# Conv gates moved to the end of each pass, parts split in place, and the last column block's weight quarters split once: a hybrid decoder step on one core

## The chip, the cores and the metric

The kernel runs on one core of a Trainium2 chip. The metric is the device time of one launch in microseconds, lower is better. TensorE (PE) does the matmuls, and its weight loads (PEld) overlap them; VectorE (DVE), ScalarE (ACT) and GpSimd (POOL) do the elementwise work; the transfers are issued on SyncE's queue (SP).

## What is computed

One layer of a decoder for 1024 prompt tokens and 64 sample tokens (8 sequences of 8), model width 2048. One input projection feeds three groups of heads; their results are joined and projected back:

```python
proj = jnp.einsum("bld,de->ble", x, w_in)
glu_a, glu_b, conv_gate, qkv, dn_gate, beta_in, decay_in, mem_q, mem_gate = jnp.split(proj, splits, axis=-1)
# conv group, 512 channels
hc, conv_state = causal_dwconv(glu_a * jax.nn.sigmoid(glu_b), conv_prev, conv_w)     # width 31
out_conv = jax.nn.silu(layer_norm(hc + conv_b, conv_ln_g, conv_ln_b)) * jax.nn.silu(conv_gate)
# delta-rule group, 8 heads of 128: short conv, gated delta rule, gated norm -> out_dn
# memory group, 4 heads of 128 over 256 memory tokens
p = jax.nn.softmax(jnp.einsum("blhd,bmhd->bhlm", mq, mem_k) * MEM_HEAD_DIM ** -0.5, axis=-1)
out_mem = jnp.einsum("blhm,bmhd->blhd", p, mem_v) * jax.nn.silu(mem_gate)
h = jnp.einsum("ble,ed->bld", jnp.concatenate([out_conv, out_dn, out_mem], axis=-1), w_out)
y = layer_norm(DEEPNORM_ALPHA * x + h, ln_g, ln_b)
```

The prompt's memory keys and values are themselves two projections (2048 to 512) of 256 memory tokens; the sample's come from a cache. The last conv rows, the delta states and the memory keys and values are outputs too.

## The kernel before, in words

Every large product is made of three matmuls on fp32r parts: a value is split into a rounded high part (an ACT copy) and the low rest (a DVE subtraction), and high x high, high x low and low x high are summed in PSUM. Weights come as raw tiles of 128 x 1024 (512 KB, a pool of 5, `rawp`), and `split_quarter` splits them in quarters of 128 x 512 into a ring of WB = 4 pairs (`wh`, `wl`); `ensure(n)` keeps n quarters split ahead of PE. The order of all loads is one list, `seq`, and a new load is issued when a raw tile is done.

**Passes.** The input projection runs twice over 52 columns of 128 outputs: pass 0 for 512 prompt tokens and the 64 samples (two banks of 288), pass 1 for the other 512 tokens. `ct_order` gives the order: 32 columns of the eight delta heads (k, q, v, gate each), 8 GLU columns (32 to 39), 4 conv gates (40 to 43), 4 memory queries (44 to 47), 4 memory gates (48 to 51). `gemm` emits a column; `finish` empties its PSUM banks behind the first matmul of the next and starts what hangs on it. Before column 44 of pass 0 `run_mem` projects the memory tokens: 192 matmuls on 32 quarters, and four more raw tiles that are split as well (`load_mem`). Pass 1 reads the keys and values back before its column 44 (`reload_mem`).

**Side work.** What follows the projection (delta chain, conv, attention) is a set of Python generators in `Side`. `tick`, called between groups of matmuls, takes them in turn and emits their next steps between PE's matmuls, if a planner's model of the engines' clocks (`Model`, `Proxy`) thinks that their inputs are there. `drain(cond)` ticks until a condition holds, without further matmuls of the column. All that is emitted is then fixed: each engine runs its instructions in this order. The conv (`gen_cgroup`) makes 31 tap instructions on DVE for each of four channel groups (with another 31 for the samples in pass 0), and holds back while the planned DVE clock is more than 1200 ns ahead of PE's. `gen_cln` then normalizes over the four groups' results `hc`, applies the gates `("g", j)`, and hands each to `put_mixed`. `gen_att` does a memory head: scores, softmax, product, for pass 0 also the samples against four cached key tiles (`kts`) and value tiles (`vts`); it multiplies by its gate and calls `put_mixed`.

**Buffers.** Most of these tiles share one pool of NW = 20 buffers (`W`, 128 x 576). Side work asks with `room(n)`, which as a rule leaves one free (KEEP); `finish` asks with `need()`, which drains side work until one is free, for each gate and query column. PSUM has four banks for columns (`m`) and four for side work (`s`).

**put_mixed** splits a finished result m of one of 16 groups into two new W tiles, high and low, and stores both to a DRAM tile `mixd[p][k]`, from where `load_mixed` brings them as stationary operands for the output.

**Output projection.** Two halves g (five tiles of tokens, the fifth the samples; then four), each in four column blocks cb of 512, 16 steps k each, three matmuls per tile and step (`out3`). `open_out`, at step 12 of the first block, drains all side work, frees the working pools and opens the output's (`Y`, among it 8 row buffers `y` of 128 x 2048). At a block's end `residual` adds alpha * x; `gen_ln` collects statistics, and after the fourth block normalizes in four pieces of 512 columns. After block 0 of the second half all side work is drained before the residuals. The last block of the second half is run in two phases: tiles 0 and 1 with all 16 steps, then tiles 2 and 3 with the same weights loaded and split again; of these the last HOLD = 10 steps are kept (six of them in `y` buffers, four in the ring), done for tile 2 first and then for tile 3. `finish_out` ends tiles 2 and 3 with DVE, ACT and POOL.

All engine calls are made in a helper, so nearly every row names line 88.

Of the kernel before, what the change touches and what calls it, by code (L numbers as in the profile page):

```python
# [16 lines left out]
P = 128  # L17
# [6 lines left out]
HOLD = 10  # L24
WB = 4
KEEP = 1
NSPLIT = 4 * 2 * 52 + 32 + 9 * KT
# [136 lines left out]
def hybrid_step(ctx, tc, I, O):  # L164
# [100 lines left out]
    for t in range(1, 52):  # L265
        if t == 44:
# [7 lines left out]
    seq += wo + wo + wo[24:]  # L274
# [46 lines left out]
    def split_quarter():  # L321
# [696 lines left out]
    convst = [dict(), dict()]  # L1018

    def gen_cgroup(p, j, a_sb, sg, psl):  # L1020
# [40 lines left out]
        for t in range(31):  # L1061
            while md.clk["DVE"] > md.clk["PE"] + 1200:
                yield "B"
# [349 lines left out]
    def run_mem(prev_fin):  # L1413
# [3 lines left out]
        bank = [(pss if i > 1 else psm).tile([P, 512], F32, tag="mmss"[i], name=nm("mm")) for i in range(4)]  # L1417
        for i in range(8):
# [18 lines left out]
            fr(2)  # L1437
        need(4)
# [53 lines left out]
    for t in range(1, 52):  # L1492
        if t == 44:
            run_mem(fin)
            fin = None
# [5 lines left out]
        fin = gemm(0, t, fin, refill_b if t == 51 else (lambda q: load_mem() if q == 2 else None) if t == 43 else None)  # L1501

    side.add(gen_gates(1, pb))
    for t in range(52):
        if t == 44:
# [59 lines left out]
    def gen_ln(rows, cb, st, y, bst, dst):  # L1565
# [6 lines left out]
        for cb in range(4):  # L1572
            cs = slice(512 * cb, 512 * cb + 512)
# [3 lines left out]
            yield  # L1577
            dve.tensor_tensor(out=yc, in0=yc, in1=gc, op=ALU.mult)
# [4 lines left out]
    def finish_out(ys, bst, xt, bank):  # L1583
        def chunk(i, cb):
            cs = slice(512 * cb, 512 * cb + 512)
            return ys[i][:, cs], Y["g"][:, cs], Y["b"][:, cs], O["y_p"][512 + i * P:512 + i * P + P, cs]

        def normalize(i, cbs):
            for cb in cbs:
                yc = chunk(i, cb)[0]  # L1590
                act.activation(out=yc, in_=yc, func=AF.Identity, scale=st[i][0], bias=st[i][1])

        def affine(i, cb, e0, e1):
            yc, gc, bb, dst = chunk(i, cb)
            e0.tensor_tensor(out=yc, in0=yc, in1=gc, op=ALU.mult)
            e1.tensor_tensor(out=yc, in0=yc, in1=bb, op=ALU.add)
            sp.dma_start(out=dst, in_=yc)

        def center(cb):
            yc, gc, bb, dst = chunk(3, cb)  # L1600
            dve.scalar_tensor_tensor(out=yc, in0=yc, scalar=st[3][2], in1=gc, op0=ALU.subtract, op1=ALU.mult)

        def rescale(cb):
            yc, gc, bb, dst = chunk(3, cb)
            dve.scalar_tensor_tensor(out=yc, in0=yc, scalar=st[3][0], in1=bb, op0=ALU.mult, op1=ALU.add)
            sp.dma_start(out=dst, in_=yc)

        st = {}
        for i in (2, 3):
            o, src = residual(P, 3, ys[i], bst[i], xt[i], bank[i])  # L1610
            dve.bn_stats(out=o, in_=src)
# [166 lines left out]
```

## Time and profile before

| what | value |
|---|---|
| runs | 2019.34, 2021.03, 4051.27 us; median 2021.03 |
| the profiled execution's own time | 2022.13 us |
| its span | 2020.4 us, 33329 instructions |
| PE busy | 1964.0 us (97%), 12172 matmuls |
| DVE, ACT, POOL busy | 1374.2 us (68%), 922.5 us (46%), 159.9 us (8%) |
| mean granted PE clock | 0.992 |
| moved by DMA | 257.35 MB, mean 127 GB/s |

How to read it: a row of the timeline gives start, length, engine, operation, output and inputs by tile names (buffer numbers left out), and in brackets how long the engine was idle before and what ended that. A row of busy times by stretch gives the stretch, its length, each engine's busy time with the number of its instructions in brackets, the granted PE clock (1.00 is full), the DMA engines' busy share and GB/s. A group row ends with busy time and mean ns, then the idle time before its members and what ended it. Tiles: `m` column banks, `mm` the memory block's, `om` the output's, `ps` side work's, `hc` the conv results.

### The profile page before, as it was taken

To read this page: it belongs to the slowest core of one execution; us is meant where nothing else is said; L and a number is where in the kernel's file an instruction comes from. 1 tells how busy PE (TensorE), PEld (TensorE's weight loads), DVE (VectorE), ACT (ScalarE), POOL (GpSimd) and SP (SyncE) were. 2 spreads that over 40 slices of the span, in tenths; PEclk is the share of its full clock that TensorE was granted. 3 is DMA by queue.
4 is the path that set the end of the run, shared out by engine and by line. 5 is a ranking of instruction groups with operands and counts; after the bars stand their busy time and mean duration, and the time that the engine had idled before them with its cause. 6 is when DMAs were issued, how large, how long until landed. Compare 5 with 4: busy or idle time off the path is not lost.

```text
span 2020.4 us, 33329 instructions
## 1 busy us (share of the span) xinstructions
PE 1964.0 (97%) x12172; PEld 1710.7 (85%) x12172; DVE 1374.2 (68%) x3423; ACT 922.5 (46%) x2279; POOL 159.9 (8%) x345
## 2 busy tenths in 40 slices
PE   8999999999999999899999999999999999999995
PEld 7999999999999979877888878888887788887784
DVE  6677767866878896455767777778995433338447
ACT  6555555555543244466545544553324522215124
POOL 6111101101101001000000000000101000000001
PEclk9999999999999999999999999999999999999998
DMA  6232333233323354374333333333332493376444
GB/s 209 85 110 74 100 110 110 73 102 110 102 95 101 99 183 131 110 231 150 120 97 99 100 99 106 110 100 95 101 115 77 139 375 103 102 245 206 140 132 150
DMA packets 114294, 257.35 MB, mean 127 GB/s; under 512 B 35281, under 2 KB 39633, under 8 KB 113873
## 3 DMA queue, kind: packets, MB, share of 16 engines
q1 hardware_dynamic: 114128, 255.22, 39.2%
q8 instruction: 96, 1.57, 0.3%
q14 instruction: 70, 0.57, 0.1%
HBM read 219.15 MB, written 36.01 MB: 126 GB/s over the span
## 4 chain that ended last, share of the span: by engine, by line
PE 44%; DVE 6%; issue 1%; ACT 1%; DMA 1%; SPq 0%; POOL 0%; DVEq 0%; ACTq 0%
PE m L88 22%; PE om L88 17%; PE ps L88 5%; DVE y L88 2%; DVE hc L88 1%; DVE wl L88 1%; DVE cv L88 1%; SPq L88 0%; DMA vts<-in_cv_dram 0%; ACT wh L88 0%; DMA ysc<-Y 0%; DVE held L88 0%; DMA mx<-mxl 0%; DMA out_y_p_dram<-y 0%; ACT gmh L88 0%
## 5 line engine op out<-in xcount | busy, mean ns | idle before, releaser
L88 PE MATMUL m<-x,wh 128*128 128x288 f32 (+1 forms) x4992 | 1228.1, 335 | 7.8 <-ACT wh L88 7.8
L88 PEld LDWEIGHTS m<-x,wh 128*128 128x128 f32 x4992 | 833.0, 189 | 84.2 <-issue 16.7
L88 PE MATMUL m<-x,wl 128*128 128x288 f32 (+1 forms) x2496 | 818.4, 328 | 1.7 <-DVE wl L88 1.7
L88 DVE TENSOR_TENSOR wl<-raw,wh 128x512 fp32r<-128x512 f32 x586 | 405.2, 698 | 294.5 <-ACT wh L88 285.6
L88 ACT CAST wh<-raw 128x512 fp32r<-128x512 f32 x586 | 357.3, 620 | 374.3 <-PE om L88 228.2
L88 PEld LDWEIGHTS m<-x,wl 128*128 128x128 f32 x2496 | 470.0, 188 | 37.4 <-DVE wl L88 2.9
L88 PE MATMUL om<-wh,x 128*128 128x512 f32 x1064 | 335.0, 391 | 0.0
L88 PEld LDWEIGHTS om<-wh,x 128*128 128x128 f32 x1064 | 200.7, 189 | 42.7 <-issue 1.0
L88 PE MATMUL om<-wl,x 128*128 128x512 f32 x564 | 220.8, 391 | 3.8 <-DVE wl L88 3.8
L88 DVE SCALAR_TENSOR_TENSOR hc<-u,cvc,hc 128x512 f32<-128x512 f32 x360 | 200.7, 595 | 2.4
L88 DVE TENSOR_TENSOR xt<-mb,X 128x8 f32<-128x8 f32 (+30 forms) x496 | 136.9, 276 | 10.5
L88 DVE SCALAR_TENSOR_TENSOR cv<-xr,qcw,cv 128x512 f32<-128x512 f32 (+1 forms) x216 | 128.9, 597 | 7.7
L88 PEld LDWEIGHTS om<-wl,x 128*128 128x128 f32 x564 | 106.5, 189 | 26.4 <-DVE wl L88 4.4
L88 ACT ACT_TABLE_LOAD x83 | 106.5, 1283 | 44.2 <-DVE smz L88 30.1
L88 DVE TENSOR_REDUCE X<-xt 128x4 f32<-128x8 f32 (+30 forms) x496 | 110.2, 222 | 10.6
L88 ACT ACTIVATE oi<-ps,GT 128x128 f32<-128x128 f32 x56 | 20.6, 368 | 210.1 <-DVE r L88 207.7
L88 ACT ACTIVATE jk<-ps 128x128 f32<-128x128 f32 x128 | 33.3, 275 | 51.8 <-PE ps L88 51.7
L88 ACT COPY xr<-m 128x288 f32<-128x288 f32 (+3 forms) x96 | 33.3, 396 | 20.5 <-PE m L88 20.0
L88 ACT ACTIVATE cv<-cv 128x512 f32<-128x512 f32 x48 | 30.3, 631 | 19.5 <-DVE cv L88 19.2
L88 PEld LDWEIGHTS ps<-S,cv 128*128 128x128 f32 x224 | 32.0, 190 | 4.7 <-DVE S L88 2.2
L88 PE MATMUL ps<-S,cv 128*128 128x128 f32 x224 | 34.4, 276 | 1.1 <-DVE S L88 1.1
L88 DVE SCALAR_TENSOR_TENSOR y<-xt,om 128x512 f32<-128x512 f32 (+1 forms) x36 | 24.2, 682 | 16.4 <-PE om L88 13.7
(318 smaller groups left out, 1817.4 us busy)
## 6 DMA issues: line engine op xcount, KB each, us to landing
raw<-in_wt_dram SPq DMA_DIRECT2D x208, 512.0 KB, 3.8
raw<-in_wo_dram SPq DMA_DIRECT2D x72, 512.0 KB, 3.9
x<-mx SPq DMA_DIRECT2D x16, 576.0 KB, 8.2
mb<-ysc SPq DMA_DIRECT2D x128, 64.0 KB, 2.2
mx<-mxh SPq DMA_DIRECT2D x32, 256.0 KB, 4.8
mx<-mxl SPq DMA_DIRECT2D x32, 256.0 KB, 4.9
xt<-in_xp_dram SPq DMA_DIRECT2D x32, 256.0 KB, 4.4
x<-mx SPq DMA_DIRECT2D x16, 512.0 KB, 3.6
```

The lines of the kernel that those rows point to most:

```text
L88: r = fn(**kw)
```

## The change

1. The order of columns: memory queries are now columns 40 to 43, memory gates 44 to 47, conv gates 48 to 51. The memory block, its loads, and the reload in pass 1 stand before column 40 instead of 44.
2. Within the memory block the conv taps are held back until the planned DVE clock is 500 ns behind PE's (`ahead`).
3. `put_mixed` writes the low part over m, and asks for one W buffer instead of two.
4. The last column block's weights are loaded and split once for both phases: its 16 quarters are kept, 8 in `y` buffers, 4 in the ring, 4 in raw tiles that no load needs any more. Tiles 0 and 1 take all 16 steps, then tile 2 all 16, then tile 3. That takes 8 loads of 512 KB and 16 quarters' splits out.
5. `gen_ln` normalizes in two pieces of 1024 columns, and holds back while the planned DVE clock is more than 1200 ns ahead.
6. The drain after block 0 of the second half ends with the first tile of the half before; a full drain stands after block 2. Tile 2 of the last block is ended as side work, and `finish_out` does tile 3 alone, on DVE and ACT, its last 512 columns in two halves.

```diff
-    order += [COL_CGATE + j for j in range(4)]
     order += [COL_MQ + j for j in range(4)]
     order += [COL_MGATE + j for j in range(4)]
+    order += [COL_CGATE + j for j in range(4)]
...
-        if t == 44:
+        if t == 40:
...
-    seq += wo + wo + wo[24:]
+    seq += wo + wo
...
-        j = nsplit[0] - 1 - (NSPLIT - (HOLD - WB))
-        if j < 0:
+        j = nsplit[0] - 1 - (NSPLIT - KT)
+        if j < 0 or 8 <= j < 12:
             hi, lo = (wp.tile([P, 512], F32R, tag=x, bufs=WB, name=nm(x)) for x in ("wh", "wl"))
-        else:
+        elif j < 8:
             if j % 2 == 0:
                 Y["held"] = Y["p"].tile([P, 2048], F32R, tag="y", bufs=8, name=nm("held"))
             hi, lo = (Y["held"][:, 1024 * (j % 2) + o:1024 * (j % 2) + o + 512] for o in (0, 512))
+        else:
+            assert nload[0] == len(seq)
+            t = rawp.tile([P, 1024], F32R, tag="raw", name=nm("held"))
+            hi, lo = t[:, 0:512], t[:, 512:1024]
...
-        yield from room(2)
-        parts = [W([P, NTOK[p]], F32R, name=n, held=True) for n in ("mxh", "mxl")]
-        act.copy(out=parts[0], in_=m)
-        dve.tensor_tensor(out=parts[1], in0=m, in1=parts[0].bitcast(F32), op=ALU.subtract)
-        fr()
-        yield tuple(parts)
+        yield from room(1)
+        hi = W([P, NTOK[p]], F32R, name="mxh", held=True)
+        act.copy(out=hi, in_=m)
+        parts = (hi, m.bitcast(F32R))
+        dve.tensor_tensor(out=parts[1], in0=m, in1=hi.bitcast(F32), op=ALU.subtract)
+        yield (hi, m)
...
+    ahead = [1200]
...
-            while md.clk["DVE"] > md.clk["PE"] + 1200:
+            while md.clk["DVE"] > md.clk["PE"] + ahead[0]:
                 yield "B"
...
+        ahead[0] = -500
         for i in range(8):
...
+        ahead[0] = 1200
         need(4)
...
-        for cb in range(4):
-            cs = slice(512 * cb, 512 * cb + 512)
+        for cb in range(2):
+            cs = slice(1024 * cb, 1024 * cb + 1024)
...
+            while md.clk["DVE"] > md.clk["PE"] + 1200:
+                yield "B"
...
+    def finish_out(y, bst, xt, bank):
+        o, src = residual(P, 3, y, bst, xt, bank)
+        dve.bn_stats(out=o, in_=src)
...
+        cols = [(0, 512), (512, 1024), (1024, 1536), (1536, 1792), (1792, 2048)]
...
+        center(cols[0])
+        dve.reciprocal(out=r, in_=r)
+        dve.scalar_tensor_tensor(out=nmr, in0=mean, scalar=-1.0, in1=r, op0=ALU.mult, op1=ALU.mult)
+        for c in cols[2:]:
+            yc = y[:, c[0]:c[1]]
+            act.activation(out=yc, in_=yc, func=AF.Identity, scale=r, bias=nmr)
+        for n, c in enumerate(cols):
+            yc, gc, bb = (t[:, c[0]:c[1]] for t in (y, Y["g"], Y["b"]))
+            if n < 2:
+                if n:
+                    center(c)
+                dve.scalar_tensor_tensor(out=yc, in0=yc, scalar=r, in1=bb, op0=ALU.mult, op1=ALU.add)
+            else:
+                dve.tensor_tensor(out=yc, in0=yc, in1=gc, op=ALU.mult)
+                dve.tensor_tensor(out=yc, in0=yc, in1=bb, op=ALU.add)
+            store(c)
...
+            held = []
+            for k in range(KT):
                 ensure(1)
                 w = ready.popleft()
                 ensure(3 if last else 2)
-                for i in idx:
+                for i in idx[:2] if last else idx:
                     out3(i, k, *w)
+                held.append(w)
                 side.tick()
...
+            if g and cb == 0:
+                side.drain(lambda: any(e[0] is first for e in side.q))
+            if g and cb == 2:
+                side.drain(lambda: side.q)
+            for i in idx[:2] if last else idx:
+                done(i)
+                if i == 0:
+                    first = side.q[-1][0]
             if last:
...
+                for i in (2, 3):
+                    for k in range(KT):
+                        out3(i, k, *held[k])
+                        side.tick()
+                    if i == 2:
+                        done(2)
                 side.drain(lambda: side.q)
...
+                finish_out(ys[3], bst[3], xt[3], bank[3])
             nblk += 1
```

More of the change, by code (lines that the diff above doesn't have):

```diff
@@ L1492, in hybrid_step @@
     for t in range(1, 52):
-        if t == 44:
+        if t == 40:
             run_mem(fin)
@@ L1581, in gen_ln @@
             sp.dma_start(out=dst[:, cs], in_=yc)
[L1583 to L1611, printed above, removed]
-            mv = Y["p"].tile([P, 2], F32, tag="mv", bufs=6, name=nm("mv"))
-            rs = Y["p"].tile([P, 2], F32, tag="rs", bufs=6, name=nm("rs"))
-            st[i] = r, nmr, mean = rs[:, 0:1], rs[:, 1:2], mv[:, 0:1]
-            dve.bn_aggr(out=mv, in_=bst[i])
-            act.activation(out=r, in_=mv[:, 1:2], func=AF.Sqrt, bias=Y["eps"])
-            if i == 3:
-                center(0)
-            dve.reciprocal(out=r, in_=r)
-            dve.scalar_tensor_tensor(out=nmr, in0=mean, scalar=-1.0, in1=r, op0=ALU.mult, op1=ALU.mult)
-            normalize(i, range(4) if i == 2 else (2, 3))
-            if i == 2:
-                affine(2, 0, dve, pool)
-                affine(2, 1, dve, pool)
-        center(1)
-        affine(2, 2, dve, pool)
-        rescale(0)
-        affine(2, 3, dve, dve)
-        rescale(1)
-        affine(3, 2, pool, pool)
-        affine(3, 3, dve, dve)
@@ L1639, in hybrid_step @@
         ys, bst = [None] * 5, [None] * 5
-        phases = [(cb, range(len(tiles))) for cb in range(3 + (1 - g))]
-        if g:
-            phases += [(3, range(2)), (3, range(2, 4))]
-        for cb, idx in phases:
+        for cb in range(4):
+            idx = range(len(tiles))
+            last = g == 1 and cb == 3
             if nblk:
@@ L1646, in hybrid_step @@
             bank = {}
-            for n, i in enumerate(idx):
-                tag = ("mmmss" if nblk == 0 else "mmsss")[n]
+            for i in idx:
+                tag = ("mmmss" if nblk == 0 else "mmsss")[i]
                 bank[i] = (psm if tag == "m" else pss).tile([P, 512], F32, tag=tag, name=nm("om"))
-            last = g == 1 and cb == 3 and 3 in idx
             def out3(i, k, wh, wl):
@@ L1661, in out3, with done @@
                 pe.matmul(out=b, lhsT=xh[k][:, sl], rhs=wl, start=False, stop=(k == KT - 1))
-            for k in range(KT - HOLD if last else KT):
+            def done(i):
+                o, rows = tiles[i]
+                if cb == 0:
+                    ys[i] = Y["p"].tile([P, 2048], F32, tag="y", bufs=8, name=nm("y"))
+                    bst[i] = Y["p"].tile([P, 4, 6], F32, tag="bst", bufs=10, name=nm("bst"))
+                if rows == 64:
+                    side.add(gen_sample(cb, ys[i], bst[i], xt[i], bank[i]))
+                    return
+                st = residual(rows, cb, ys[i], bst[i], xt[i], bank[i])
+                side.add(gen_ln(P, cb, st, ys[i], bst[i], O["y_p"][g * 512 + o:g * 512 + o + P, :]))
+            held = []
+            for k in range(KT):
                 ensure(1)
@@ L1674, in hybrid_step @@
                     load_mixed(1, k)
-            if last:
-                held = []
-                for k in range(KT - HOLD, KT):
-                    ensure(1)
-                    held.append(ready.popleft())
-                    out3(2, k, *held[-1])
-                    ensure(2)
-                    side.tick()
-                side.drain(lambda: side.q)
-                for k in range(KT - HOLD, KT):
-                    out3(3, k, *held[k - KT + HOLD])
-                finish_out(ys, bst, xt, bank)
-                break
-            if g and cb == 0:
-                side.drain(lambda: side.q)
-            for i in idx:
-                o, rows = tiles[i]
-                if cb == 0:
-                    ys[i] = Y["p"].tile([P, 2048], F32, tag="y", bufs=8, name=nm("y"))
-                    bst[i] = Y["p"].tile([P, 4, 6], F32, tag="bst", bufs=10, name=nm("bst"))
-                if rows == 64:
-                    side.add(gen_sample(cb, ys[i], bst[i], xt[i], bank[i]))
-                else:
-                    st = residual(rows, cb, ys[i], bst[i], xt[i], bank[i])
-                    side.add(gen_ln(P, cb, st, ys[i], bst[i], O["y_p"][g * 512 + o:g * 512 + o + P, :]))
+            if g and cb == 0:
[6 more added lines that the diff above has]
+                    first = side.q[-1][0]
+            if last:
+                for i in (2, 3):
[4 more added lines that the diff above has]
+                        done(2)
+                side.drain(lambda: side.q)
+                finish_out(ys[3], bst[3], xt[3], bank[3])
             nblk += 1
```

17 lines of the change are left out of this document (13 added, 4 removed).

## The prediction

> **What bounds the kernel now.** I read the page first, then the busy times in stretches cut where a column of weights, the memory block or an output block begins (found by counting matmuls in the timeline: 96 a column in pass 0, 48 in pass 1, 224 and 192 an output block), then the waits of PE, then the timeline where a stretch is longer than its matmuls explain.
>
> ```profile
> span 2020.4 us, 33329 instructions
> PE 1964.0 (97%) x12172; PEld 1710.7 (85%) x12172; DVE 1374.2 (68%) x3423; ACT 922.5 (46%) x2279; POOL 159.9 (8%) x345
> ```
>
> PE is busy 97% of the span, and the change takes no matmul away and adds none. So nothing can be won but PE's idle time (2020.4 - 1964.0 = 56 us, the tail included) and what a lowered clock costs behind it. The profiled execution took 2022.13 us around this span; it stands 1.1 us above the median of 2021.03. The sum is made against 2022.1.
>
> ```profile
> core 0: us, PE busy (x) PEld busy (x) DVE busy (x) ACT busy (x) POOL busy (x), PEclk, DMA share, GB/s
> 651.60:702.50 50.90, 50.90 (x386) 50.90 (x385) 46.82 (x101) 14.05 (x25) 1.35 (x4) 1.00 0.35 110
> 715.30:763.80 48.50, 45.51 (x194) 35.87 (x194) 47.11 (x95) 23.42 (x41) 0.03 (x1) 1.00 0.59 195
> 342.00:359.90 17.90, 17.90 (x150) 17.44 (x146) 11.05 (x45) 7.56 (x19) 1.04 (x6) 1.00 0.53 171
> 834.50:862.40 27.90, 22.55 (x146) 18.35 (x145) 10.23 (x24) 12.86 (x27) 0.00 (x0) 0.88 0.39 130
> ...
> 1405.90:1420.20 14.30, 14.30 (x79) 12.11 (x78) 13.57 (x28) 3.16 (x7) 0.55 (x1) 1.00 0.24 76
> 1575.60:1598.90 23.30, 20.12 (x78) 14.53 (x77) 7.76 (x20) 10.53 (x27) 0.00 (x0) 0.85 0.14 46
> 1861.70:1911.80 50.10, 46.35 (x193) 37.84 (x192) 23.83 (x38) 9.92 (x16) 0.00 (x0) 0.93 0.49 156
> 1911.80:1955.40 43.60, 43.60 (x194) 36.08 (x193) 15.99 (x25) 10.06 (x17) 0.00 (x0) 1.00 0.37 121
> 1955.40:2002.70 47.30, 44.71 (x193) 35.49 (x191) 37.97 (x66) 23.85 (x40) 0.00 (x0) 1.00 0.50 172
> 2002.70:2020.40 17.70, 0.01 (x1) 0.00 (x0) 12.75 (x17) 4.75 (x7) 7.92 (x5) 0.62 0.34 119
> ```
>
> The reader is to compare stretches with equally many matmuls. 651.6 is four undisturbed columns of pass 0, 1911.8 an undisturbed output block of the second half: 43.6 us, 0.225 us a matmul. Six stretches stand out: the memory block (715.3: 48.5 us for the same 194 matmuls), column 49 of pass 0 (834.5: 27.9 us where column 20, at 342.0 with 150 matmuls, took 17.9), column 50 of pass 1 (1575.6: 23.3 against the 14.3 of 1405.9), the second block of the second half (50.1), its last block (47.3), and 17.7 us after the last matmul. Excess: 4.9, 10.0, 9.0, 6.5, 3.7 us and the tail. These are the six places that the change touches.
>
> **The tail (A).** Now tile 2 and tile 3 end 4 us apart and their normalization shares DVE; afterwards tile 3 alone is left.
>
> ```profile
> 2005.08 0.68 DVE L88 SCALAR_TENSOR_TENSOR y<-xt,om 128x512 f32<-128x512 f32 x1
> 2005.80 0.69 DVE L88 BATCH_NORM_STATS2 bst<-y 128x6 f32<-128x512 f32 x1
> 2006.53 0.27 DVE L88 BATCH_NORM_AGGREGATE mv<-bst 128x2 f32<-128x24 f32 x1
> ...
> 2007.98 0.15 DVE L88 RECIPROCAL rs<-rs 128x1 f32<-128x1 f32 x1
> 2008.17 0.16 DVE L88 SCALAR_TENSOR_TENSOR rs<-mv,rs 128x1 f32<-128x1 f32 x1
> 2008.24 0.75 DVE L88 SCALAR_TENSOR_TENSOR y<-y,mv,lng 128x512 f32<-128x512 f32 x1
> ...
> 2010.17 1.75 DVE L88 TENSOR_TENSOR y<-y,lng 128x512 f32<-128x512 f32 x1
> ...
> 2015.89 0.69 DVE L88 TENSOR_TENSOR y<-y,lnb 128x512 f32<-128x512 f32 x1
> ```
>
> Tile 3's residual begins at 2005.08, 2.4 us after its last matmul, because tile 2's chain stands ahead of it; 512 columns cost 0.68 to 0.75 us, and 1.75 us where POOL works beside DVE (the row at 2010.17; the change uses POOL no more here). New chain on DVE by starts: residual 0.72, statistics 0.73, aggregate 0.30, first centring 0.75 (it covers ACT's square root), reciprocal and shift 0.38, rescale, centre, rescale 2.2, one column block multiplied and added 1.4, two half blocks, not in this trace, between 0.35 (half) and 0.69 (whole) an instruction, taken at 0.42 as nearer the half, four of them 1.7. That is 8.2, and 0.3 to begin, and 3.8 from DVE's end (2015.89 + 0.69) to the span's end: 12.3. Tiles 0 to 2 need some 7 us of DVE each, 21 us inside the 22 us of tiles 2 and 3's matmuls, so up to 3 us of backlog; I take 1. Tail 13.3, **gain 4.4** (2.4 to 5.4).
>
> **The last block (B).** Now weight quarters that are to be kept are split between normalization steps, and PE waits for them; the memory block waits for splits too:
>
> ```profile
> PE mm L88 <- DVE wl L88: 3.0, 3, 1.4
> PE om L88 <- DVE held L88: 2.6, 3, 1.0
> ...
> L88 DVE TENSOR_TENSOR wl<-raw,wh 128x512 fp32r<-128x512 f32 x586 | 405.2, 698 | 294.5 <-ACT wh L88 285.6
> L88 ACT CAST wh<-raw 128x512 fp32r<-128x512 f32 x586 | 357.3, 620 | 374.3 <-PE om L88 228.2
> ```
>
> After it, sixteen quarters are split during tiles 0 and 1 and kept, and tiles 2 and 3 run on splits that are done. A quarter must come every 6 x 0.225 = 1.35 us; ACT needs 0.62 and DVE 0.70, so PE is fed, once the four residuals of the block before are through. The sixteen splits and eight loads of 512 KB that go away were under PE's work; they are worth nothing by themselves. Of 3.7 I take **3.3** (1.2, if the residuals and statistics at the start hold splits back by 2.5, to 3.9).
>
> **The drain after the first block of the second half (C).** Now every generator is emptied there: the normalization steps still left run on DVE before the four residuals that free the PSUM banks, PE stands idle 50.1 - 46.35 = 3.75 us, and the clock of the stretch falls to 0.93. With the change only tile 0 of the half before is drained, the first in the list and a whole block old; its buffer is the one that the new tile 3 needs. **6.5** (0 to 6.6); the price, if its cover is gone, is today's stall. The other tiles go on in the next block, where DVE is 24 of 50 us busy. Of the 6.5, 3.75 are idle time and 2.75 the lower clock. The Trainium skill (TensorE: Matmul & The Clock Gate, What's actually happening) says that an idle window of 3.4 us halves the clock for at least one busy window; one window at half speed would cost 1.7 us, not the 2.75 of this row, and the sum would be 1 us smaller for each stall removed.
>
> **The memory block (D).** It is fed 32 quarters, 22 us of DVE, and conv taps are put between them:
>
> ```profile
> 560.00:664.40 104.40, 40.33 (x89) 0.00 (x0) 0.00 (x0) 1.00 0.30 96
> 664.40:715.30 50.90, 32.63 (x74) 0.00 (x0) 0.00 (x0) 1.00 0.31 101
> 715.30:763.80 48.50, 26.48 (x58) 0.00 (x0) 0.03 (x1) 1.00 0.59 195
> ```
>
> These are the instructions on tile hc (column 2 is DVE). With the limit at -500 a tap is issued only while the plan has DVE behind PE, so 26.5 us of taps mostly leave the 48.5 (DVE 47.1 busy). **3.5** of 4.9 (0, where the planner's clock misjudges, to 4.9). But the block also moves four columns ahead, to about 664. There 89 of 248 taps are done; some 140 are left after it, at 74 in 51 us some 97 us: the taps end near 805, where now 27 are left at 763.8, and the normalization over channels follows: 61 us now from its sum (765.3) to the first gated block (826.2), by the first starts in these rows on hc:
>
> ```profile
> L88 DVE TENSOR_TENSOR mxl<-hc,mxh x8: 680/721/761, 826.2 to 1624.1; 128x576 fp32r<-128x576 f32 x4, 128x512 fp32r<-128x512 f32 x4
> ...
> L88 POOL TENSOR_TENSOR lsum<-lsum,hc x4: 1420/1440/1587, 765.3 to 1526.4; 128x576 f32<-128x576 f32 x2, 128x512 f32<-128x512 f32 x2
> ```
>
> So the gated blocks fall to 866 and later, beside the conv gates at columns 48 to 51; a conv gate that comes sooner only holds a buffer longer.
>
> **The end of each pass (E, F).** Stalls there come from the shared pool of 20 W buffers. A gate column asks for a buffer and, if none is free, side work is put out until one is; PE's queue then holds that side work ahead of the next column:
>
> ```profile
> 837.82 1.74 PE L88 MATMUL ps<-kts,dgq 128*32 128x256 f32 x12 [0.95 <-DMA kts<-in_ckT_dram]
> 842.79 0.66 PE L88 MATMUL ps<-ident,pt 128*128 128x128 f32 x2 [3.23 <-DVE pt L88]
> ```
>
> PE waits for the loads of one attention head and then for its softmax, with nothing between. Counted from the code: now, at the first memory gate, four each are held by memory, conv results, conv gates and memory queries, 16 of 20, and a head of pass 0 needs six. With the conv gates last, 12 are held when the memory gates come, attention has run since the queries' first column, and a head's query and gate are free as soon as it is done; each mixed output asks for one buffer where it asked for two. When the conv gates come (columns 48 to 51) heads 0 to 2 should be gone. I take **8** of 10.0 in pass 0 and **7** of 9.0 in pass 1 (from -10 and -9, a second stall of the same price, to 10 and 9). The conv results' stores come later, but they are read only from the last output block of the first half on. Reloading the memory keys in pass 1 (four transfers on SP) moves ahead with the queries.
>
> Splitting in place (the low part over m) costs nothing more: the same instruction, and its next writer is far. Halves of 1024 columns instead of quarters in the block normalization save a fixed part of DVE time that nobody waits for.
>
> **Sum.** 4.4 + 3.3 + 6.5 + 3.5 + 8 + 7 = 32.7; 2022.1 - 32.7 = 1989.4, and 1.1 less as a median: **1988 us**, faster by 1.6%.
>
> **Rivals.**
> - Everything at its upper bound: 5.4 + 3.9 + 6.6 + 4.9 + 10 + 9 = 39.8, and some 3 us of lowered clock in the columns behind the two stalls (an estimate by the 2.75 of C): 43, **1978 us**. For it: no stretch has another bound than PE. Against: each replacement starts with a cold pipeline somewhere.
> - The stalls only move: attention at columns 41 to 47 competes with taps for DVE (46.8 of 50.9 busy at 651.6), heads fall behind their gates, and one gate per pass still drains. E and F are 0: 2022.1 - 17.7 = 2004.4, **2003 us**.
> - The conv tail reaches the opening of the output phase, which empties all side work in the first output block (its first instruction stands below; 1648 now, 1629 with D, E and F won). From the last sum to the last conv block it takes 98 us in pass 1 now (1526.4 to 1624.1 above); if attention delays the taps by a column (14 us, the row at 1405.9), the tail ends near 1638, a stall of 9: **1997 us**.
>
> ```profile
> 1647.91 0.10 POOL L1525 MEMSET epsc<- 128x1 f32 x1 [90.79 <-DMA raw<-in_wo_dram]
> ```
>
> - Slower: all four memory gates of each pass find no buffer, since taps and heads both hold theirs. Three more stalls of 10.0 and three of 9.0 are 57, against the 17.7 of A to D: 2061. It decides from two stalls on (19 us). Against: side work must leave one buffer free until the channel normalization begins, so a first gate finds one. What else makes heads slow are the table loads, each on the way from scores to probabilities; with four of them a head spends 5 us of ACT on them:
>
> ```profile
> L88 ACT ACT_TABLE_LOAD x83 | 106.5, 1283 | 44.2 <-DVE smz L88 30.1
> ```
>
> The Trainium skill (ScalarE: Activation LUTs, Table sets: the hidden batching unit) tells to batch calls by function set, against which this order mixes heads, gates and conv normalization. With the 2.66 us that it gives for a switch, four would be some 11 us. ACT is 12.9 of 27.9 us busy in the row at 834.5, so neither changes the sum.
>
> **How the numbers follow.** Forecast 0.50, all at the bound 0.20, moved stalls 0.17, conv tail 0.08, slower 0.05. The range 1975 to 2011 holds the first four nearly whole. About 2% (40 us, under 1981) is what a measurement here tells from no change: below it lies most of the second case, 0.16; over 2061 about half of the last, 0.03; within, 0.81.
>
> **What would show it.** Right: memory block near 44 to 45 us; second block of the second half near 43.6 with clock 1.00; last block under 45 with no wait for held; tail 12 to 14 with POOL idle; no column over 20 us in pass 0's last twelve, or over 17 in pass 1's. Wrong: PE idle times over 3 us with a lowered clock at columns 44 to 51, PE waiting near the opening of the output phase, or a matmul rate that changed somewhere else.

## The result, and the profile after

The changed kernel takes **1988.54 us** (median of 4, from 1988.34 to 1988.8) beside 2020.18 us for the kernel before on the same chip: a ratio of 0.9851, with a 95% interval from 0.9835 to 0.9867. One of the four runs of the kernel before took 4051.27 us; the ratio goes by fast runs alone, so it is not the quotient of the two medians. Its profiled execution took 1988.42 us around a span of 1986.7 us, so the two profiled spans differ by 33.7 us.

The first lines of the page of the changed kernel:

```profile
span 1986.7 us, 33145 instructions
...
PE 1951.6 (98%) x12172; PEld 1706.3 (86%) x12172; DVE 1358.6 (68%) x3382; ACT 908.0 (46%) x2249; POOL 156.9 (8%) x340
```

The matmuls are the same 12172. Outside PE's busy time 35.1 us of the span are left, where there were 56.4; that is 21.3 of the 33.7. The other 12.4 lie in PE's busy time itself, which the lowered clock had stretched behind three stalls: three times the 2.75 of the prediction are some 8 of it, and the rest was not followed.

The busy times of the changed kernel by stretch, cut at the same matmuls as before. The columns are start and end, length, then busy time and count for PE, PEld, DVE, ACT and POOL, then the granted clock, the DMA share and GB/s. In order: the memory block; columns 40 to 51 of pass 0; its columns 49 and 51 alone; columns 0 to 33 of pass 1; columns 40 to 51 of pass 1, and column 50 alone; the second and the last block of the second half; the tail.

```profile
663.90:709.20 45.30, 45.16 (x193) 35.94 (x193) 42.25 (x83) 23.33 (x40) 3.17 (x4) 1.00 0.69 229
709.20:903.50 194.30, 191.34 (x1426) 173.99 (x1424) 133.71 (x277) 93.70 (x192) 10.34 (x8) 1.00 0.50 156
848.60:868.00 19.40, 18.76 (x135) 16.26 (x133) 13.44 (x22) 14.68 (x28) 2.99 (x2) 1.00 0.52 152
883.90:903.50 19.60, 18.68 (x131) 13.68 (x129) 13.38 (x22) 12.07 (x22) 0.00 (x0) 1.00 0.91 293
903.50:1368.90 465.40, 461.30 (x2585) 378.95 (x2584) 334.50 (x971) 239.73 (x658) 32.77 (x70) 1.00 0.33 101
1443.70:1595.10 151.40, 151.07 (x661) 120.85 (x660) 108.35 (x181) 68.09 (x135) 11.62 (x8) 1.00 0.40 127
1573.40:1584.20 10.80, 10.80 (x49) 8.97 (x48) 5.82 (x9) 5.52 (x9) 0.00 (x0) 1.00 0.68 215
1844.10:1887.60 43.50, 43.50 (x193) 36.05 (x192) 20.76 (x31) 11.11 (x17) 0.00 (x0) 1.00 0.55 177
1931.20:1975.60 44.40, 44.40 (x193) 35.80 (x191) 31.25 (x47) 10.84 (x14) 0.00 (x0) 1.00 0.26 95
1975.60:1986.70 11.10, 0.00 (x0) 0.00 (x0) 7.55 (x16) 2.09 (x4) 0.00 (x0) 0.69 0.38 142
```

The three stretches of the kernel before that answer to the long ones here and were not shown: columns 44 to 51 of pass 0 (columns 40 to 43 were the 50.9 us from 664.4, with 386 matmuls), columns 0 to 33 and columns 40 to 51 of pass 1.

```profile
763.80:902.50 138.70, 132.67 (x941) 118.13 (x939) 74.62 (x143) 66.14 (x136) 8.76 (x8) 0.98 0.48 151
902.50:1379.40 476.90, 474.47 (x2685) 385.57 (x2684) 342.76 (x999) 252.26 (x689) 32.24 (x70) 1.00 0.35 110
1454.20:1612.70 158.50, 154.21 (x662) 122.34 (x661) 106.62 (x175) 65.96 (x131) 10.43 (x8) 0.98 0.31 103
```

Every stage clock that was 0.85 to 0.98 is now 1.00. Stretch by stretch, in us (from the starts of the matmuls, so a length can differ by 0.1 from the rows, which are cut at tenths):

| stretch | before | after | won | forecast |
|---|---|---|---|---|
| memory block (D) | 48.5 | 45.4 | 3.1 | 3.5 |
| pass 0, columns 40 to 51 | 189.6 | 194.2 | -4.6 | 8 (E) |
| pass 1, columns 0 to 33 | 476.9 | 465.4 | 11.5 | 0 |
| pass 1, columns 40 to 51 (F) | 158.5 | 151.4 | 7.1 | 7 |
| second block of the second half (C) | 50.1 | 43.5 | 6.6 | 6.5 |
| last block (B) | 47.3 | 44.4 | 2.9 | 3.3 |
| tail (A) | 17.7 | 11.1 | 6.6 | 4.4 |
| all else | | | 0.5 | 0 |

The total is what was forecast, but the surprise stands in rows 2 and 3. The columns that were to win 8 us became 4.6 us longer, and 11.5 us are gone behind them, at the start of pass 1 (10.2 of the 11.5 in its first ten columns, which took 139.9 and take 129.7). The count of matmuls tells what happened: 99 more stand in pass 0's columns 40 to 51 (1426 against 386 + 941), and exactly 100 fewer in pass 1's first 34 columns (2585 against 2685). By their tiles these 100 are all matmuls of attention heads, side work that used to spill over the boundary of the passes.

So the two rows have to be read together, since work that has moved is not work that is won. In columns 0 to 33 of pass 1, PE's busy time fell by 13.2 us (474.5 to 461.3) while its idle time rose from 2.4 to 4.1. In columns 40 to 51 of pass 0 its busy time rose by 7.8 us (183.6 to 191.3) and its idle time fell from 6.0 to 3.0. Together the two stretches went from 666.6 to 659.7 us: 6.9 us are won, beside the 8 of E. Only 1.4 of them are idle time; the rest is busy time, some 2.75 of it the clock behind the stall by the prediction's reading, and what is left was not followed.

PE's list of waits has lost the entries for held quarters, for the memory block's splits and for the 3.8 us of the second block; what is left in the changed kernel is spread out (engine, tile and the tile it waited for; us in total, times, longest):

```profile
PE m L87 <- ACT wh L87: 9.3, 2, 7.9
PE ps L87 <- DVE ut L87: 3.8, 7, 1.4
PE ps L87 <- DVE S L87: 1.7, 2, 0.9
...
PE ps L87 <- DVE pt L87: 0.6, 2, 0.3
```

The first row is the start of the kernel for 7.9 of its 9.3 us (7.4 before); the wait for a softmax (pt) was 6.8 us, 3.2 at the longest.

### The profile page after: what moved, and what is told of

The parts are those of the page before. It is cut to its first block, busy times and chain, and to the rows that moved or that the text cites. A ratio compares the mean times of both kernels' runs of the same rounds, so it can differ in the third digit from the quotient of the medians.

```text
span 1986.7 us, 33145 instructions
## 1 busy us (share of the span) xinstructions
PE 1951.6 (98%) x12172; PEld 1706.3 (86%) x12172; DVE 1358.6 (68%) x3382; ACT 908.0 (46%) x2249; POOL 156.9 (8%) x340
## 4 chain that ended last, share of the span: by engine, by line
PE 87%; DVE 7%; ACT 4%; DMA 1%; issue 1%; POOL 0%; SPq 0%; DVEq 0%; ACTq 0%
PE m L87 55%; PE om L87 19%; PE ps L87 11%; DVE cv L87 2%; PE mm L87 2%; DVE wl L87 1%; DMA raw<-in_wt_dram 1%; ACT wh L87 1%; ACT L87 1%; DVE xt L87 1%; DVE hc L87 0%; DVE X L87 0%; DVE S L87 0%; ACT jk L87 0%; ACT gmh L87 0%
## 5 line engine op out<-in xcount | busy, mean ns | idle before, releaser
L87 PEld LDWEIGHTS m<-x,wh 128*128 128x128 f32 x4992 | 831.6, 189 | 86.1 <-issue 14.6
L87 DVE TENSOR_TENSOR wl<-raw,wh 128x512 fp32r<-128x512 f32 x564 | 388.1, 694 | 266.6 <-ACT wh L87 257.8
L87 ACT CAST wh<-raw 128x512 fp32r<-128x512 f32 x564 | 343.3, 619 | 307.4 <-PE om L87 219.1
L87 PE MATMUL om<-wh,x 128*128 128x512 f32 x992 | 311.1, 390 | 0.0
L87 PEld LDWEIGHTS om<-wh,x 128*128 128x128 f32 x992 | 185.9, 188 | 39.4 <-issue 1.0
L87 PE MATMUL om<-wl,x 128*128 128x512 f32 x528 | 205.5, 389 | 0.0
L87 ACT ACTIVATE oi<-ps,GT 128x128 f32<-128x128 f32 x56 | 20.6, 368 | 214.2 <-DVE r L87 212.0
L87 PEld LDWEIGHTS om<-wl,x 128*128 128x128 f32 x528 | 99.1, 188 | 20.7
## 6 DMA issues: line engine op xcount, KB each, us to landing
x<-mx SPq DMA_DIRECT2D x16, 576.0 KB, 11.1
```

The lines of the kernel that those rows point to most:

```text
L87: r = fn(**kw)
```

## The experiments

Twelve kernels ran. Each is compared with the kernel before on the same chip (2019.7 to 2021.1 us), and with the changed kernel by its profiled span. None leaves out a part of the computation. The theory from the prediction is that the stalls at the end of each pass are a shortage of W buffers (E, F), that the stall in the second output block is the full drain (C), and that the memory block is slow because of taps (D). The rivals are named with each run.

**Part 1 alone: the new order of columns, in the kernel before.**

```diff
-    order += [COL_CGATE + j for j in range(4)]
     order += [COL_MQ + j for j in range(4)]
     order += [COL_MGATE + j for j in range(4)]
+    order += [COL_CGATE + j for j in range(4)]
...
-        if t == 44:
+        if t == 40:
```

> The kernel before with part 1 of the change alone: conv gates last, memory block, its loads and the reload four columns earlier; everything else as before. Buffer theory: the stalls at the end of each pass come where a gate finds none of the 20 W buffers free and side work is put out in one go. The program counts its free buffers as it is built: before, none at the first memory gate of pass 0 and at the second and third of pass 1; in this order never none. So column 49 of pass 0 and column 50 of pass 1 lose their stalls, the pass boundary gains about 7 us and the end of pass 1 about 7: 2020 - 14 = 2006. The memory block stays near 48.5, the drain, last block and tail as before. Rival (the in-place split frees the buffers, the order only moves the stalls): two stalls of 9 to 10 us at columns 44 to 47, 2018 to 2022.

Measured: 2011.92 us, ratio 0.9963 (0.9950 to 0.9975). Columns 40 to 51 of pass 0, columns 0 to 33 and columns 40 to 51 of pass 1:

```profile
714.70:912.20 197.50, 192.82 (x1425) 174.04 (x1423) 127.43 (x261) 94.33 (x192) 9.91 (x8) 1.00 0.49 153
912.20:1377.60 465.40, 461.34 (x2586) 378.87 (x2585) 334.71 (x971) 239.80 (x658) 32.26 (x70) 1.00 0.33 101
1452.40:1604.40 152.00, 151.10 (x661) 120.82 (x660) 108.95 (x181) 68.10 (x135) 11.59 (x8) 1.00 0.40 127
```

The order by itself moves the 100 matmuls (1425 and 2586) and ends the stall of column 50 (6.5 of the 7.1 us). At the boundary of the passes it wins less than the expected 7: the two stretches together take 662.9 us, 3.7 less than before, and the memory block takes 1 us more. PE's idle time in the two is even a little longer (8.7 us against 8.5), but no row has a lowered clock any more. Columns 46 and 47 of pass 0 take 19.4 and 20.0 us, the place that the rival named, at a smaller price.

**One more W buffer, in the kernel before.** The space comes from one buffer of another tile.

```diff
-    NW, NX, NU, N5, NZ = 20, 1, 2, 17, 12
+    NW, NX, NU, N5, NZ = 21, 1, 2, 17, 12
...
-            Sn = wk.tile([P, P], F32, tag="S", bufs=NH + 2, name=nm("S"))
+            Sn = wk.tile([P, P], F32, tag="S", bufs=NH + 1, name=nm("S"))
```

> The kernel before with nothing of the change, but 21 W buffers instead of 20 (one of the ten delta-state buffers given up for the space). Buffer theory: by the program's count the first memory gate of pass 0 now finds a buffer, while three gates of pass 1 still find none; so column 49 of pass 0 falls from 27.9 to some 18 to 19, pass 1's columns 48 to 50 keep about 10 us of stalls, and the time is 2011 to 2015. Rival (heads are simply late for their gates in the old order, buffers or not): column 49 keeps its 27 to 28 us and the time stays 2018 to 2022.

Measured: 2028.87 us, ratio 1.0052 (1.0034 to 1.0070): slower, against the expectation. Column 49 of pass 0, then columns 0 to 33 of pass 1:

```profile
849.80:864.10 14.30, 14.30 (x114) 13.32 (x113) 7.01 (x13) 8.01 (x14) 0.00 (x0) 1.00 0.93 287
...
905.30:1385.10 479.80, 472.53 (x2663) 386.04 (x2660) 342.58 (x994) 248.44 (x682) 31.34 (x70) 0.99 0.34 104
```

The stall of column 49 is gone with the 21st buffer (14.3 us at a full clock, from 27.9), so a lack of buffers did cause it. But pass 1 begins with 19.2, 18.6, 15.2 and 14.6 us in its first four columns. Columns 40 to 51 of pass 0 together with columns 0 to 33 of pass 1 take 663.7 us, 2.8 less than before, and PE is idle for 9.0 us of them, where it was idle for 8.5: the wait had moved across the boundary. The loss lies elsewhere, the largest part in columns 0 to 39 of pass 0 (6.6 us). It may come from the buffer given up for the 21st; this was not separated, so the time of this run does not say what a buffer more is worth.

**Part 3 alone: the low part written in place, in the kernel before.**

```diff
-        yield from room(2)
-        parts = [W([P, NTOK[p]], F32R, name=n, held=True) for n in ("mxh", "mxl")]
+        yield from room(1)
+        hi = W([P, NTOK[p]], F32R, name="mxh", held=True)
...
```

> The kernel before with part 3 alone: the low part is written over m and one W buffer is asked for instead of two. Buffer theory with the program's count: pass 0's gate at column 48 still finds none and drains as long as before, pass 1 drains once instead of twice; column 49 of pass 0 stays near 28 and pass 1's end gains 0 to 4: 2016 to 2020. Rival (fewer buffers asked for is what ended the stalls): both gone, 2006.

Measured: 2020.11 us, ratio 1.0002 (0.9993 to 1.0012). Column 49 still takes 28.1 us, and columns 50 and 51 of pass 1 20.6 and 16.1. One buffer less for each mixed output does not open these stalls; as the count in the expectation says, the gate at column 48 of pass 0 still finds none free.

**All but part 1: the changed kernel with the old order of columns** (the first diff turned round).

> The changed kernel with part 1 undone: old order, memory block before column 44, everything else changed. Theory that the order ends the stalls: both come back, 1988.5 + 14 = 2002. Buffer theory with the program's count: pass 0 never finds the pool empty here either (conv taps are held back in the memory block, and each result asks for one buffer), pass 1 drains briefly behind columns 3 and 48; so most of the 14 stays, 1990 to 1995, and column 49 of pass 0 is below 21.

Measured: 2001.04 us, ratio 0.9913 (0.9897 to 0.9929); the span is 12.6 us above the changed kernel's. Columns 49 and 51 of pass 0, and columns 0 to 33 of pass 1:

```profile
831.80:844.50 12.70, 12.70 (x98) 12.70 (x98) 8.19 (x13) 6.47 (x12) 0.00 (x0) 1.00 0.69 206
860.00:893.70 33.70, 25.24 (x155) 16.67 (x151) 19.70 (x38) 23.92 (x47) 0.97 (x2) 0.92 0.57 182
893.70:1381.30 487.60, 480.53 (x2727) 388.88 (x2725) 337.66 (x978) 261.01 (x705) 29.17 (x70) 1.00 0.37 111
```

This run tells the two readings of E apart. Parts 2 and 3 by themselves leave column 49 without any stall (12.7 us, its 98 matmuls back to back), as the buffer theory said. But 8.5 us of idle time then stand in column 51, where the second half's input is loaded (33.7 us against 25.2 busy), and 142 more matmuls than in the changed kernel fall into the first 34 columns of pass 1. From column 40 of pass 0 to column 33 of pass 1, PE is idle for 15.6 us here and for 7.1 in the changed kernel. So the stall that the prediction priced is not what the order is worth: the order gets attention done before the passes meet. PE's waits in column 51 of this run say what is late there:

```profile
PE ps L87 <- DVE pt L87: 4.9, 2, 3.2
PE bd L87 <- DMA raw<-in_xb_dram: 3.5, 2, 2.7
```

A head's softmax, and the loads of the second half's input. The first half's output also took 3.6 us more here. That is not the conv tail: PE is busy all through it (208.5 of 208.5 us), and 16 matmuls of an attention head stand in it that pass 1 has in the changed kernel.

**Parts 4 to 6 alone: the output phase of the changed kernel, with both passes as before.**

> The kernel before with the output part of the change alone (parts 4, 5 and 6; parts 1 to 3 undone). If the six gains are separate, it gains what the two traces show there: second block of the second half 6.6, last block 2.9, tail 6.6, together 16: 2020 - 16 = 2004, with the stalls of columns 49 and 50 as before. Rival (the output part hangs on the earlier end of the side work): less than 12, over 2008.

Measured: 2005.12 us, ratio 0.9925 (0.9910 to 0.9940). Second block 43.5, last block 44.4, tail 11.1 us, each as in the changed kernel, while columns 49 and 50 stall as before (26.8 and 23.2). The two halves of the change do not touch one another: A to C are won here alone.

**The full drain put back, in the changed kernel.**

```diff
-                side.drain(lambda: any(e[0] is first for e in side.q))
+                side.drain(lambda: side.q)
```

> The changed kernel with one line of part 6 undone: all side work is drained after block 0 of the second half. The prediction's theory (the drain itself puts the normalization ahead of the residuals): the stall of before is back, second block 50, 1988.5 + 6.5 = 1995. Rival by the trace of the changed kernel: only one piece of 1024 columns, 2.4 us of DVE, is left there, because the two-piece normalization of part 5 is through sooner; a stall of 1 to 3 us, second block 44 to 47, 1989 to 1992.

Measured: 1990.78 us, ratio 0.9856 (0.9842 to 0.9871). The second block:

```profile
1845.30:1889.70 44.40, 43.81 (x193) 35.95 (x192) 20.79 (x31) 9.99 (x17) 0.00 (x0) 1.00 0.53 175
```

It takes 0.9 us more, not the 6.5 of the forecast. In this kernel little is left for the full drain: one piece of 64 rows, 2.4 us of DVE, as the rival said. Whether the drain did more with the normalization of before is asked next.

**The normalization in four pieces, without the hold (part 5 undone)**, once with the short drain of the change (four_pieces) and once with the full one as well (four_pieces_drain).

```diff
-        for cb in range(2):
-            cs = slice(1024 * cb, 1024 * cb + 1024)
+        for cb in range(4):
+            cs = slice(512 * cb, 512 * cb + 512)
...
-            while md.clk["DVE"] > md.clk["PE"] + 1200:
-                yield "B"
```

> The changed kernel with part 5 alone undone: four pieces of 512 columns, the short drain kept. If the short drain ends the stall by itself, second block 43.5 to 44.5, and the time 1988 to 1990, the tail up to 1.5 us longer by DVE's backlog (four pieces cost a tile about 0.4 us more of DVE). If the pieces alone ended it, 49 to 50, 1994 to 1996.

> The changed kernel with the full drain of before after block 0 of the second half and the normalization in four pieces of 512 columns without the hold (part 5 undone). Theory after drain_all (the shorter normalization, not the drain, ended the stall): second block 49 to 50.5, 1994 to 1996. Rival (neither matters, the stall went with the earlier end of the first half): under 46, 1991.

Measured: 1995.37 us (ratio 0.9879, 0.9864 to 0.9895) and 1996.46 us (0.9882, 0.9866 to 0.9898). The second block of the first, then of the second:

```profile
1845.20:1894.30 49.10, 45.35 (x193) 37.09 (x192) 23.84 (x38) 9.91 (x17) 0.00 (x0) 0.97 0.50 159
```

```profile
1845.40:1895.60 50.20, 46.45 (x194) 37.96 (x193) 23.91 (x38) 9.96 (x17) 0.00 (x0) 0.93 0.47 157
```

PE stands idle for 3.75 us in both, as long as before the change: with four pieces the short drain wins nothing of it. PE's only wait in that block, first before the change, then with four pieces and the short drain:

```profile
PE om L88 <- DVE wl L88: 3.8, 1, 3.8
```

```profile
PE om L87 <- DVE wl L87: 3.7, 1, 3.7
```

So PE does not wait for a PSUM bank that the residuals free, as the prediction had it, but for the low part of a weight quarter: the block's first two steps run at once, and the split for the third comes late. DVE's timeline at the start of that block shows why (start, duration, tiles and shape), first with four pieces and the short drain, then in the changed kernel:

```profile
1845.21 0.68 DVE L87 TENSOR_TENSOR y<-y,lng 128x512 f32<-128x512 f32 x1
...
1851.23 0.69 DVE L87 TENSOR_TENSOR y<-y,lnb 64x512 f32<-64x512 f32 x1
1851.84 2.46 DVE L87 SCALAR_TENSOR_TENSOR y<-xt,om 128x512 f32<-128x512 f32 x4
1854.23 1.88 DVE L87 TENSOR_TENSOR wl<-raw,wh 128x512 fp32r<-128x512 f32 x3
```

```profile
1844.64 0.68 DVE L87 TENSOR_TENSOR wl<-raw,wh 128x512 fp32r<-128x512 f32 x1
1845.24 2.46 DVE L87 SCALAR_TENSOR_TENSOR y<-xt,om 128x512 f32<-128x512 f32 x4
1847.63 1.27 DVE L87 TENSOR_TENSOR wl<-raw,wh 128x512 fp32r<-128x512 f32 x2
...
1851.81 1.21 DVE L87 TENSOR_TENSOR y<-y,lng 64x1024 f32<-64x1024 f32 x1
```

With four pieces, five products and five sums, 6.6 us of DVE, stand ahead of the four residuals, and the splits follow only at 1854.23. Counted as the two kernels are built, four of the ten instructions are put out with the last matmuls of block 0, and six by the drain, by the short one just as by the full one: it serves all tiles in turn until the first is done, and by then the others have put out theirs. With part 5 the residuals come first, the splits follow at 1847.63, and one tile's piece of 64 rows comes after them. Whether the size of the pieces or the hold does it was not separated.

**Taps as before in the memory block (part 2 undone), and taps held back longer**, in the changed kernel.

```diff
-        ahead[0] = -500
+        ahead[0] = 1200
```

> The changed kernel with part 2 undone: the limit stays 1200 ns in the memory block. Theory that the limit feeds the splits: the memory block goes from 45.4 back to 48.5 to 50, the time to 1991 to 1994. Rival (the four columns' earlier place made it shorter): block stays 45 to 46, time within 1 of 1988.5.

Measured: 1996.21 us, ratio 0.9882 (0.9867 to 0.9896). The memory block with all instructions, then with those on tile hc alone (column 2 is DVE), then the changed kernel's on hc:

```profile
664.60:714.20 49.60, 45.56 (x195) 35.88 (x194) 48.98 (x99) 23.45 (x41) 1.92 (x4) 1.00 0.64 208
...
663.90:713.50 49.60, 27.12 (x60) 0.00 (x0) 0.00 (x0) 1.00 0.64 209
```

```profile
663.90:709.20 45.30, 20.07 (x44) 0.00 (x0) 0.00 (x0) 1.00 0.69 229
```

At the block's new place part 2 is worth 4.2 us in the block, and 3.1 in columns 40 to 51, which neither side expected. But 44 of the 60 instructions on hc are still in the block; most of them were not taken out.

```diff
-        ahead[0] = -500
+        ahead[0] = -1500
```

> The changed kernel with the conv taps held back by 1500 ns instead of 500 in the memory block. If bursts of taps ahead of splits are what is left there (45.4 against 43.6), the block comes to 43.5 to 44.7 and the time to 1986.5 to 1988; taps pushed behind the block may cost up to 2 us at the end of pass 0. If the four loads of memory tokens and their splits make the rest, the block stays at 45 to 45.6.

Measured: 1990.5 us, ratio 0.9852 (0.9834 to 0.9870). The block stays at 45.4 us, with 38 instructions on hc in it, and columns 40 to 51 take 196.0, 1.8 more. So the 1.8 us that the block has above the 43.6 of an output block are not bursts of taps. They are no wait at all: the changed kernel's row has PE busy for 45.16 of its 45.30 us. Why the matmuls of this block take longer than those of the output stays open.

**Two W buffers in the mixed output (part 3 undone), in the changed kernel** (the diff of part 3 turned round).

> The changed kernel with part 3 undone: the low part in a tile of its own, two W buffers asked for. Buffer theory: by the program's count no gate finds the pool empty in this kernel either, so nothing to gain: 1988 to 1990. Rival (one buffer less is what lets the results of both groups leave in time at the end of pass 0): columns 45 to 47 of pass 0 near 20 as with the order alone, 1992 or more.

Measured: 1990.28 us, ratio 0.9853 (0.9836 to 0.9869); the span is 1.4 us longer, 1.0 of it in columns 40 to 51 of pass 0 and 0.7 in those of pass 1. That is little, and a span of one execution at that; with the new order the second buffer is hardly missed. The rival is out as well: columns 45 to 47 take 15.4, 15.2 and 17.3 us. With part 2 undone (ahead_same) columns 46 and 47 take 19.4 and 19.3, so part 2 is what shortened them.

**Part of the tail on POOL, in the changed kernel**: the last 512 columns' product and sum on POOL, and their stores ahead of the others.

```diff
-        for n, c in enumerate(cols):
+        for n, c in [(3, cols[3]), (4, cols[4]), (0, cols[0]), (1, cols[1]), (2, cols[2])]:
...
-                dve.tensor_tensor(out=yc, in0=yc, in1=gc, op=ALU.mult)
-                dve.tensor_tensor(out=yc, in0=yc, in1=bb, op=ALU.add)
+                e = dve if n == 2 else pool
+                e.tensor_tensor(out=yc, in0=yc, in1=gc, op=ALU.mult)
+                e.tensor_tensor(out=yc, in0=yc, in1=bb, op=ALU.add)
```

> The changed kernel with the last 512 columns of the last tile multiplied and added on POOL instead of DVE, and begun first. DVE has 1.7 us less to do: if POOL and DVE work side by side without harm, the tail falls from 11.1 to 9.4 to 10. By the rows of the kernel before, where DVE's steps took 1.63 to 1.75 us beside POOL instead of 0.69, four or five slowed steps cost 4 us: tail 11.5 to 14, 1989 to 1991.

Measured: 1991.18 us, ratio 0.9857 (0.9841 to 0.9873); the tail takes 13.7 us. DVE's steps beside POOL, and POOL's last:

```profile
1979.61 1.10 DVE L87 SCALAR_TENSOR_TENSOR y<-y,rs,lnb 128x512 f32<-128x512 f32 x1
1980.63 1.21 DVE L87 TENSOR_TENSOR y<-y,lng 128x512 f32<-128x512 f32 x1
1981.87 1.09 DVE L87 TENSOR_TENSOR y<-y,lnb 128x512 f32<-128x512 f32 x1
...
1982.50 1.05 POOL L87 TENSOR_TENSOR y<-y,lnb 128x256 f32<-128x256 f32 x1
```

DVE's 512 columns go from 0.69 to some 1.1 to 1.2 us, yet both engines are through by 1983.55, when DVE alone in the changed kernel is through at 1983.42. The end comes 5.6 us after that, not 3.3. SP puts out its stores in the order written, and here the first two wait for POOL, so the others are late although their data is not: the last store is put out at 1984.97, in the changed kernel at 1983.45. That the order of the stores makes the difference is argued from these times; the same work with the stores in another order was not run.

## Why the prediction was right in the total, and where its steps failed

The forecast of 1988 us for the median was met (1988.54), and the sum of 32.7 against a span that is 33.7 us shorter. The steps stand less well than the sum.

- **Bound: right.** PE's work is the bound, and what was won is its idle time, the lowered clock behind it, and a few us of its busy time that were not followed. No stage of the table has another bound.
- **A, the tail: mis-sized.** 6.6 won against 4.4, beyond its upper bound of 5.4. The chain on DVE, from the last residual to the last half block, was right to 0.4 us, the halves at 0.42 us exactly as taken:

```profile
1974.40 1.22 DVE L87 TENSOR_TENSOR y<-y,lnb 128x1024 f32<-128x1024 f32 x1
1975.63 0.69 DVE L87 SCALAR_TENSOR_TENSOR y<-xt,om 128x512 f32<-128x512 f32 x1
...
1983.00 0.42 DVE L87 TENSOR_TENSOR y<-y,lnb 128x256 f32<-128x256 f32 x1
```

  It begins at 1975.63 and ends at 1983.42: 7.8 against 8.2. Tile 2's last piece ends at 1975.62, just as the last matmul does, so there is no backlog (1 was taken) and no start (0.3), and from DVE's end to the end of the span it takes 3.3, not 3.8. The bound on the gain counted on at least no backlog and kept the other two fixed; it should have let them move.
- **B, the last block: right**, 2.9 against 3.3; output_only gives it alone.
- **C, the second output block: the size right, the steps wrong.** "Now every generator is emptied there" is true, and of the ten instructions that stand ahead of the residuals the drain puts out six. But the stall is a wait for a weight split behind them in DVE's queue, not for the PSUM banks. And the step that was to end it failed: "The other tiles go on in the next block" does not hold for the short drain, which with four pieces puts out the same six and leaves 5.6 us of the 6.5 (four_pieces). Part 5, which the prediction priced as "a fixed part of DVE time that nobody waits for", is what removed the stall; with it, even the full drain costs only 0.9. The two errors cancelled, and that the term fits is luck.
- **D, the memory block: nearly right**, 3.1 against 3.5, but the 4.9 that it was taken from was no measure of the wait. PE was idle for 3.0 us of the block before (48.5 against 45.5 busy), and all of this is won; the rest is the pace of the block's own matmuls. The taps did not "mostly leave" it either: 44 stayed, where it had 58. In the changed kernel these cost PE no wait in the block, and undoing part 2 brings back 4.0 us of waits for splits with 60 of them; that it is bursts of taps that harm is argued. Part 2 also helped the columns after the block, which the prediction did not see: ahead_same is 7.9 us longer in span.
- **E, the end of pass 0: the size nearly right, its parts not.** 6.9 us were won at the boundary of the passes (11.5 - 4.6), for the 8 that were taken. The cause of the stall in column 49 was named rightly: one more buffer ends it, and so do parts 2 and 3. The step that failed is "I take 8 of 10.0", which took the whole stall as the price of its removal. 5.4 us of the stalled column were idle time (27.9 against 22.55 busy), but over both stretches the idle time fell by 1.4 only, and in one_more_buffer and all_but_order, which have no stall in column 49, it rose. Other waits took its place. What is gone is the lowered clock, and 5.4 us of busy time altogether, more than the clock explains. That the two errors leave a sum near 8 is in part luck.
- **F, the end of pass 1: right**, 7.1 against 7: of columns 40 to 51 the idle time fell from 4.3 to 0.3 us and the busy time from 154.2 to 151.1. The order alone gives 6.5 of it.
- **The rivals.** The stalls moved as a whole only in kernels without the new order. The conv tail reached the opening of the output phase in none of the kernels that are shown here. The slower rival did not show: no wait of PE but the kernel's start is over 1.4 us. Of what the prediction named as signs, the tail came out under its 12 to 14 us and the memory block, at 45.4, just over its 44 to 45; the others hold, and no column of pass 0's last twelve exceeds 19.6 us.

## What to carry to other kernels

Where side work is woven into a bound engine's queue, a stall is often only the place at which overdue work is paid for: before pricing its removal, count the side instructions on either side of the next boundary, and add up the stretches between which they move. A drain is judged by what it puts out, and a shorter condition may put out just as much; what counts is how much is left when it is reached, so the pace of the steps before it matters more. To learn what an engine waits for, read the wait itself: here it was a weight split that stood far back in another engine's queue. And at the end of a kernel it is worth asking whether the order of the stores in one queue holds back data that is ready.

## What the runs showed of the hardware

After the same gap, the clock was lowered for 3.4 us in one kernel and for twice as long in the other. PE's waits in the second output block of the kernel before and with four pieces are equally long (3.75 us of idle time). The stretches behind them, first before, then with four pieces (column 8 is the granted clock):

```profile
1871.00:1876.00 5.00, 4.53 (x11) 3.56 (x12) 4.59 (x8) 0.28 (x1) 0.00 (x0) 0.50 0.86 271
1876.00:1881.00 5.00, 5.00 (x21) 4.09 (x20) 1.39 (x2) 0.96 (x2) 0.00 (x0) 0.89 0.40 134
```

```profile
1855.00:1860.00 5.00, 5.00 (x15) 3.97 (x16) 4.70 (x8) 0.62 (x1) 0.00 (x0) 0.66 0.81 234
1860.00:1865.00 5.00, 5.00 (x24) 4.15 (x23) 0.78 (x2) 1.25 (x2) 0.00 (x0) 1.00 0.79 257
```

In the first the records hold the clock at 0.5 for 6.827 us, in the second for 3.413. With equal idle time, PE's busy time for the block is 46.35 us in the one and 45.35 in the other, so a window more costs 1.0 us here. The Trainium skill (TensorE: Matmul & The Clock Gate, What's actually happening) speaks of windows of some 3.4 us, with the full clock back after at least one busy window: the length agrees with the 3.413, and in the clock records of all these kernels, of the 15 stalls ahead of the tail that lowered the clock, six kept it low for one window, eight for two and one (inplace_only, in column 49) for three. The 2.75 us that the prediction took for the clock from the trace is that of two windows.

A two-input DVE instruction on 512 columns takes 0.69 us alone, 1.63 to 1.75 beside POOL's instructions on 512 columns (before the change), and 1.09 to 1.21 beside POOL's on 256 (with part of the tail on POOL): the price goes with what POOL is doing, and is not one figure.
